# Differential heads: the last keys of a tile by two F32R products of stacked parts, and the norm's squares added by halves

## The chip, the cores and the metric

The kernel runs on one core of one Trainium2 chip. Its engines are named as in the profile: PE is TensorE (the matrix products; PEld is its weight load), DVE is VectorE, ACT is ScalarE, POOL is GpSimd, and SP issues most of the transfers. The metric is the device time of one execution in microseconds (us), as the median of several runs.

## The reference

One block of a streaming encoder, in float32, on 512 tokens of 1024 channels with 16 meta tokens ahead of them (528 positions). The part that matters here is the second branch, differential attention with 8 heads of value width 128:

```
s = einsum('bhcqd,bhckd->bhcqk', q, k) * 64 ** -0.5      # two maps c per head
p = softmax(where(mask, s + bias, -inf))
w = p[:, :, 0] - lam * p[:, :, 1]
o = einsum('bhqk,bhkd->bhqd', w, v)
o = rmsnorm(o, subln_g) * (1 - lam_init)                 # per head and token, over the 128 channels
```

The mask is causal by chunks of 64 tokens. A tile of 128 query tokens therefore sees all positions up to its own end. Since the 16 meta tokens shift the positions, the last 16 keys of a tile lie in the next block of 128 positions, and only the upper 64 query rows of the tile see them. Before this branch comes stick-breaking attention (also 8 heads), and after both a gated merge, an output projection, a SwiGLU and a last norm.

## The kernel before

**Precision.** A product with FP32 operands and one with F32R operands (float32 rounded to a shorter form) are different instructions for TensorE. Nearly all products of the kernel are therefore made in F32R by thirds (`mm3`, L293): each operand is cut into a high part (a copy that rounds, on ACT) and a low part (operand minus high part, on DVE or POOL), and high x high, high x low and low x high are added in PSUM. `split` (L77) makes such a pair: the cast goes to ACT (L78), the subtraction to the engine named (L81). A few small products are left in FP32.

**Order of the work.** Per branch, the heads run in a loop (L1001). A head is a generator (`df_head`, L685) that yields between its steps; at each yield, units of the next head's projections, of finished output projections (`y_units`, L770) and the turning of the next head's values (`turn`, L530) are put in. So PE has other products while the softmax of the head runs on ACT and DVE. Weights come in chunks by SP, are split by ACT and DVE two chunks ahead in this branch (`weights`, L284), and wait in a few buffers. Partial sums of the output projection leave by transfers that POOL issues (L787, L789); POOL also issues the transfers that add weight blocks in the background (L151), one at a time, each behind the last cast made so far. Within these bounds a scheduler orders the instructions of each engine by priority, which follows the program, and by readiness.

**One differential head.** `scores` (L702) and `scores3` (L711) make the logits per query tile, `maps` (L718) the two softmax maps and their difference, in `prs[t]`, queries on partitions. `attn_out` (L550) then has two steps. `turned` transposes the weights' blocks on PE (L563, L564), so that keys lie on partitions; three blocks are cut into high and low parts (L568, L569), the fourth stays FP32 (`a_f`, L570). The last 16 keys of each tile are handled apart: DVE transposes blocks of 32 x 32 (L574), whose last 16 columns are those keys, into `a_s`, which has 32 partitions and 64 columns for each tile. `weighted` adds up the output in one PSUM bank: nine F32R products (L582), one FP32 product of 128 columns with `a_f` (L583), and one FP32 product of 256 columns with `a_s` (L584), which writes the upper 64 columns of each of the four tiles. Its values come from `turn`: `v_s` holds the last 16 positions of each tile in the last 16 of 32 columns, and is transposed on PE (L544) and copied out (L545). The stick-breaking heads use the same functions with 32 query rows instead of 64 (`lo_rows` 96 instead of 64).

**The head's norm.** The output, 128 channels on partitions and 512 tokens in columns, is copied out of PSUM (L751). Its squares are made by POOL (L753), in the last head by DVE, and split into `sqh` (ACT) and `sql` (POOL or DVE) at L754. `norm` (L756) runs inside the next head, after that head's first two score tiles and one unit: two products with a matrix of 1/128 (`ones_r`) add the squares over the partitions (L758, L759), and ACT and DVE make the inverse root and scale the output (L760 to L765). The last head's norm runs after the loop (L1040).

Of the kernel before, what the change touches and what calls it, by code (L numbers as in the profile page):

```python
# [9 lines left out]
F32 = mybir.dt.float32  # L10
F32R = mybir.dt.float32r
BF16 = mybir.dt.bfloat16
AF = mybir.ActivationFunctionType
ALU = mybir.AluOpType
AX = mybir.AxisListType

P = 128
D = 1024
SEQ = 512
NM = 16  # L20
L = NM + SEQ
# [3 lines left out]
NH = 8  # L25
# [16 lines left out]
def block_kernel(ctx: ExitStack, tc: tile.TileContext, x, meta, norm_mix_g, w_in, w_gate, b_gate,  # L42
# [484 lines left out]
    def v_units(key, d):  # L527
        vT = d["vT"] = ap_.tile([P, L], F32, tag="vT", bufs=1, name="vT")

        def turn():  # L530

            vf = ap_.tile([P, 2, P], F32, tag="vf", bufs=2, name="vf")
            vh = ap_.tile([P, 3, P], F32R, tag="vh", bufs=2, name="vh")
            vl = ap_.tile([P, 3, P], F32R, tag="vl", bufs=2, name="vl")
            pt, p5 = tr_tile(), tr_tile()
            for j in range(4):
                nc.tensor.transpose(pt[:, j * P:(j + 1) * P], vT[:, j * P:(j + 1) * P], ident)  # L537
            pv = pt.rearrange("p (j c) -> p j c", c=P)
            nc.scalar.copy(vh, pv[:, 0:3])
            nc.vector.tensor_tensor(vl, pv[:, 0:3], vh.bitcast(F32), op=ALU.subtract)  # L540
            nc.scalar.copy(vf[:, 0], pt[:, 3 * P:4 * P])
            nc.scalar.copy(v_s.rearrange("p (t q) -> p t q", q=32)[:, :, 32 - NM:32],
                           vT[:, NM:L].rearrange("p (t q) -> p t q", q=P)[:, :, P - NM:P])
            nc.tensor.transpose(p5[:, 0:P], v_s, ident)  # L544
            nc.scalar.copy(vf[:, 1], p5[:, 0:P])  # L545
            d["v"] = (vf, vh, vl)

        return kv_units(key, lambda ps, s: nc.scalar.copy(vT[:, s], ps)), turn

    def attn_out(blocks, d, lo_rows):  # L550

        qn = P - lo_rows
        off = (0, 512, 896)
        a_h = ap_.tile([P, 1152], F32R, tag="a_h", name="a_h")
        a_l = ap_.tile([P, 1152], F32R, tag="a_l", name="a_l")
        a_f = ap_.tile([P, P], F32, tag="a_f", name="a_f")

        def turned():
            z0, z1 = z_tile(), z_tile()
            banks = z0[:, 0], z1[:, 0], z0[:, 1]  # L560
            for j, pt in enumerate(banks):
                for t in range(j, NQ):
                    nc.tensor.transpose(pt[:, (t - j) * P:(t - j + 1) * P], blocks(t, j * P, (j + 1) * P), ident)  # L563
            nc.tensor.transpose(z1[:, 1, 0:P], blocks(3, 3 * P, 4 * P), ident)  # L564
            for j, pt in enumerate(banks):
                n = 512 - j * P
                c = slice(off[j], off[j] + n)
                nc.scalar.copy(a_h[:, c], pt[:, 0:n])  # L568
                nc.vector.tensor_tensor(a_l[:, c], pt[:, 0:n], a_h[:, c].bitcast(F32), op=ALU.subtract)  # L569
            nc.scalar.copy(a_f, z1[:, 1, 0:P])  # L570
            for t in range(NQ):
                b = blocks(t, (t + 1) * P - 32 + NM, (t + 1) * P + NM)
                for i in range(qn // 32):
                    nc.vector.transpose(a_s[32 * t:32 * t + 32, t * qn + 32 * i:t * qn + 32 * i + 32],  # L574
                                        b[lo_rows + 32 * i:lo_rows + 32 * i + 32])

        def weighted():
            vf, vh, vl = d["v"]
            ps = z_tile()[:, 0]
            for j in range(3):  # L580
                n = 512 - j * P
                mm3(ps[:, j * P:512], [(vh[:, j], vl[:, j], a_h[:, off[j]:off[j] + n], a_l[:, off[j]:off[j] + n])], j == 0, False)  # L582
            nc.tensor.matmul(ps[:, 3 * P:512], lhsT=vf[:, 0], rhs=a_f, start=False, stop=False)  # L583
            nc.tensor.matmul(ps.rearrange("p (t q) -> p t q", q=P)[:, :, lo_rows:P], lhsT=vf[:, 1],  # L584
                             rhs=a_s[:, 0:4 * qn], start=False, stop=True)
            return ps

        return turned, weighted


# [94 lines left out]
    def df_head(h, d, o_h, o_l):  # L685
        q, k = d["q"], d["k"]
        bias = ap_.tile([P, L], F32, tag="bias", name="bias")
        nc.gpsimd.tensor_scalar(bias, dist, -(2.0 ** -(h + 1)), None, op0=ALU.mult)
        mx = small.tile([P, NQ, 2], F32, tag="mx", name="mx", bufs=2)
        ls = small.tile([P, NQ, 2], F32, tag="ls", name="ls", bufs=2)  # L690
        prs = [ap_.tile([P, 2, 144 + t * P], F32, tag=f"w{t}", name="pr") for t in range(NQ)]

        def score(o, t, c, k0, k1):
            qs = slice(t * P, (t + 1) * P)
            nc.tensor.matmul(o, lhsT=q[c][:, qs], rhs=k[c][:, 0, k0:k1], start=True, stop=False)  # L695
            nc.tensor.matmul(o, lhsT=q[c][:, qs], rhs=k[c][:, 1, k0:k1], start=False, stop=True)  # L696

        def biased(t, c, zz, po, bb):
            nc.vector.tensor_tensor_reduce(po, zz, bb, scale=1.0, scalar=-3.0e38, op0=ALU.add, op1=ALU.max,  # L699
                                           accum_out=mx[:, t, c:c + 1])  # L700

        def scores(t):  # L702
            n = 144 + t * P
            z = z_tile()
            for c in range(2):
                score(z[:, c, 0:max(n, 256)], t, c, 0, max(n, 256))
            for c in range(2):
                biased(t, c, z[:, c, 0:n], prs[t][:, c], bias[:, L - n:L])
            maps(t)

        def scores3(c):  # L711
            two = lambda v: v.rearrange("p (a b) -> p a b", a=2)
            z = z_tile()
            for hf in range(2):
                score(z[:, hf, 0:HL], 3, c, hf * HL, (hf + 1) * HL)
            biased(3, c, z[:, :, 0:HL], two(prs[3][:, c]), two(bias))

        def maps(t):  # L718
            pr = prs[t]
            nm = small.tile([P, 2], F32, tag="nm", name="nm")  # L720
            nc.vector.tensor_scalar(nm, mx[:, t], -1.0, None, op0=ALU.mult)
            for c in range(2):
                nc.scalar.activation(pr[:, c], pr[:, c], AF.Exp, bias=nm[:, c:c + 1], accum_out=ls[:, t, c:c + 1])
            with tc.high_priority(offset=EVAC):
                rc = small.tile([P, 2], F32, tag="rc", name="rc")
                nc.vector.reciprocal(rc, ls[:, t])
                nc.vector.tensor_tensor(rc, rc, cn, op=ALU.mult)
                nc.vector.tensor_scalar(pr[:, 0], pr[:, 0], rc[:, 0:1], None, op0=ALU.mult)
                nc.vector.scalar_tensor_tensor(pr[:, 0], pr[:, 1], rc[:, 1:2], pr[:, 0], op0=ALU.mult, op1=ALU.add)

        scores(0)
        scores(1)
        yield 1
        if late:
            late.pop(0)()
        scores(2)
        yield 1
        scores3(0)
        yield 1
        scores3(1)  # L740
        maps(3)
        turned, av = attn_out(lambda t, k0, k1: prs[t][:, 0, k0:k1], d, 64)
        yield 3 if h < NH - 1 else 2
        turned()
        yield 2
        ps = av()
        of = ap_.tile([P, SEQ], F32, tag="of", name="of")
        sq = ap_.tile([P, SEQ], F32, tag="sq", name="sq")
        sqh = ap_.tile([P, SEQ], F32R, tag="a_h", name="sqh")
        sql = ap_.tile([P, SEQ], F32R, tag="a_l", name="sql")  # L750
        nc.scalar.copy(of, ps)  # L751
        eng = nc.gpsimd if h < NH - 1 else nc.vector
        eng.tensor_tensor(sq, of, of, op=ALU.mult)  # L753
        split(sqh, sql, sq, lo_eng=eng)  # L754

        def norm():  # L756
            pv = tr_tile()
            nc.tensor.matmul(pv, lhsT=ones_r, rhs=sql, start=True, stop=False)  # L758
            nc.tensor.matmul(pv, lhsT=ones_r, rhs=sqh, start=False, stop=True)  # L759
            nc.scalar.activation(sq, pv, AF.Ln, bias=eps_c)  # L760
            cast["norm"] = nc.scalar.activation(sq, sq, AF.Exp, scale=-0.5)
            nc.vector.scalar_tensor_tensor(sq, pv, var_max, sq, op0=ALU.is_le, op1=ALU.mult)
            nc.vector.tensor_tensor(of, of, sq, op=ALU.mult)
            nc.scalar.activation(o_h, of, AF.Copy, scale=g_sub)
            nc.vector.scalar_tensor_tensor(o_l, of, g_sub, o_h.bitcast(F32), op0=ALU.mult, op1=ALU.subtract)  # L765

        late.append(norm)


# [778 lines left out]
```

## Time and profile before

| | us |
|---|---|
| median of 3 runs (lowest to highest) | 931.77 (931.14 to 932.34) |
| the profiled execution | 931.87 |
| its span, first to last instruction | 930.1 |
| DVE busy | 734.3 |
| ACT busy | 586.1 |
| POOL busy | 168.4 |

The profile comes from one execution. Its span leaves out what lies before the first and after the last instruction (1.77 us here). An engine's busy time is the union of its instructions. In a timeline each row is a start, a length, the engine, the source line, what is written and read, and in brackets how long the engine was idle before and what ended that. In the chain of waits, PE's products stand with the time by which the next could follow; in the timeline they stand with their whole length through the array, so that neighbours overlap.

### The profile page before, as it was taken

What the parts mean: (1) busy time and instruction counts of PE and PEld (TensorE: products, weight loads), DVE (VectorE), ACT (ScalarE), POOL (GpSimd) and SP (SyncE); (2) the same over time, 40 slices, a digit from 0 to 9 for tenths busy, and PEclk for the clock granted to TensorE, in tenths of its full rate; (3) what the DMA queues carried; (4) which work ended last, traced back from release to release, by engine and by line L of the source; (5) the groups of instructions that cost most, each with busy time, mean ns of one, the idle gap of its engine ahead of it and who ended that gap; (6) DMA issues with size and microseconds to landing.
All of it is one profiled execution on the core that took longest, in us unless ns stands there. A gap on an engine that the chain in (4) does not pass through costs nothing.

```text
span 930.1 us, 16033 instructions
## 1 busy us (share of the span) xinstructions
PE 918.8 (99%) x6010; PEld 836.9 (90%) x6010; DVE 734.3 (79%) x1413; ACT 586.1 (63%) x1104; POOL 168.4 (18%) x199
## 2 busy tenths in 40 slices
PE   8999999999999999999999999999999999999997
PEld 5999999998999899998988888899999999988886
DVE  7988877776687767976663787899888888799975
ACT  6765676676666666666665555776555555576554
POOL 3000121222333343344512000001100000000013
PEclk9999999999999999999999999999999999999999
DMA  8525598778777878799987774437744343276542
GB/s 253 139 68 168 143 212 201 169 167 250 191 192 177 217 170 182 181 211 186 197 209 181 215 260 159 127 80 183 169 118 131 91 129 98 88 274 193 192 149 91
DMA packets 155823, 158.41 MB, mean 170 GB/s; under 512 B 6465, under 2 KB 117218, under 8 KB 155746
## 3 DMA queue, kind: packets, MB, share of 16 engines
q1 hardware_dynamic: 132690, 101.61, 36.2%
q0 software_dynamic: 22896, 55.72, 29.2%
q8 instruction: 47, 0.77, 0.3%
q14 instruction: 30, 0.25, 0.1%
q10 hardware_dynamic: 160, 0.07, 0.0%
HBM read 133.64 MB, written 50.86 MB: 198 GB/s over the span
## 4 chain that ended last, share of the span: by engine, by line
PE 94%; DVE 3%; ACT 2%; issue 1%; ACTq 0%; DVEq 0%
PE mm L297 22%; PE mm L296 22%; PE mm L298 22%; PE z L297 7%; PE z L296 7%; PE z L298 7%; PE z L563 2%; PE z L696 1%; PE z L695 1%; PE tr L537 1%; DVE wl L81 1%; DVE hres L1205 1%; PE z L584 1%; PE mm L858 0%; ACT wh L78 0%
## 5 line engine op out<-in xcount | busy, mean ns | idle before, releaser
L296 PE MATMUL mm<-xT_h,wh 128*128 128x264 f32 (+2 forms) x656 | 213.6, 326 | 0.5 <-ACT xT_h L901 0.5
L297 PE MATMUL mm<-xT_l,wh 128*128 128x264 f32 (+2 forms) x656 | 213.4, 325 | 0.5
L298 PE MATMUL mm<-xT_h,wl 128*128 128x264 f32 (+2 forms) x656 | 212.5, 324 | 0.0
L78 ACT CAST wh<-wst 128x1024 fp32r<-128x1024 f32 (+1 forms) x147 | 141.5, 967 | 78.8 <-PE mm L297 56.0
L81 DVE TENSOR_TENSOR wl<-wst,wh 128x1024 fp32r<-128x1024 f32 (+1 forms) x147 | 163.1, 1114 | 31.3 <-ACT wh L78 30.9
L297 PEld LDWEIGHTS mm<-xT_l,wh 128*128 128x128 f32 x656 | 123.4, 188 | 10.3 <-DVE xT_l L902 1.3
L298 PEld LDWEIGHTS mm<-xT_h,wl 128*128 128x128 f32 x656 | 123.5, 188 | 10.0
L296 PEld LDWEIGHTS mm<-xT_h,wh 128*128 128x128 f32 x656 | 123.4, 188 | 9.9 <-ACT xT_h L901 0.9
L296 PE MATMUL mm<-hT_h,wh 128*128 128x256 f32 x304 | 84.0, 278 | 0.5 <-ACT hT_h L1162 0.5
L298 PE MATMUL mm<-hT_h,wl 128*128 128x256 f32 x304 | 84.1, 278 | 0.0
L297 PE MATMUL mm<-hT_l,wh 128*128 128x256 f32 x304 | 84.1, 277 | 0.0
L699 DVE CUSTOM_DVE_ANT_0 pr<-z,bias 128x144 f32<-128x144 f32 (+3 forms) x64 | 30.9, 501 | 34.1 <-PE z L696 31.8
L296 PEld LDWEIGHTS mm<-hT_h,wh 128*128 128x128 f32 x304 | 56.9, 188 | 0.8 <-ACT hT_h L1162 0.7
L298 PEld LDWEIGHTS mm<-hT_h,wl 128*128 128x128 f32 x304 | 57.2, 188 | 0.0
L297 PEld LDWEIGHTS mm<-hT_l,wh 128*128 128x128 f32 x304 | 57.0, 188 | 0.0
L296 PE MATMUL mm<-o_h,wh 128*128 128x512 f32 x128 | 52.4, 410 | 0.0
L297 PE MATMUL z<-wl,da 128*128 128x512 f32 (+1 forms) x132 | 50.3, 381 | 0.2 <-DVE wl L81 0.2
L296 PE MATMUL z<-wh,da 128*128 128x512 f32 (+1 forms) x132 | 50.2, 380 | 0.0
L298 PE MATMUL z<-wh,da 128*128 128x512 f32 (+1 forms) x132 | 50.2, 380 | 0.0
L298 PE MATMUL mm<-o_h,wl 128*128 128x512 f32 x128 | 50.1, 391 | 0.0
L297 PE MATMUL mm<-o_l,wh 128*128 128x512 f32 x128 | 49.9, 390 | 0.0
L151 POOL DMA_DIRECT2D ds<-in_w_ffn_down_dram x36 | 30.1, 840 | 92.0 <-ACT wh L78 62.2
(378 smaller groups left out, 2468.0 us busy)
## 6 DMA issues: line engine op xcount, KB each, us to landing
wst<-in_w_in_dram SPq DMA_DIRECT2D x40, 512.0 KB, 5.9
ds<-in_w_ffn_down_dram POOLq DMA_DIRECT2D x30, 512.0 KB, 6.2
wst<-in_w_ffn_gate_dram SPq DMA_DIRECT2D x22, 512.0 KB, 3.9
wsu<-in_w_ffn_up_dram SPq DMA_DIRECT2D x20, 512.0 KB, 3.9
wst<-in_w_gate_dram SPq DMA_DIRECT2D x16, 512.0 KB, 5.5
y_df<-y_out POOLq DMA_DIRECT2D x32, 256.0 KB, 7.2
slots<-ds SPq DMA_DIRECT2D x13, 512.0 KB, 3.2
os<-in_w_out_dram POOLq DMA_DIRECT2D x12, 512.0 KB, 5.0
```

Source lines behind the costliest of these rows:

```text
L78: cast["last"] = (hi_copy or nc.scalar.copy)(hi, src)
L81: cast["lo"] = (lo_eng or nc.vector).tensor_tensor(lo, src, hi.bitcast(F32), op=ALU.subtract)
L151: tc.add_manual_dep(nc.gpsimd.dma_start(dst, src, **kw).ins, cast["last"].ins.name, paced)
L296: nc.tensor.matmul(ps, lhsT=ah, rhs=bh, start=(start and i == 0), stop=False, skip_group_check=skip)
L297: nc.tensor.matmul(ps, lhsT=ah, rhs=bl, start=False, stop=False, skip_group_check=skip)
L298: nc.tensor.matmul(ps, lhsT=al, rhs=bh, start=False, stop=(stop and i == n - 1), skip_group_check=skip)
L537: nc.tensor.transpose(pt[:, j * P:(j + 1) * P], vT[:, j * P:(j + 1) * P], ident)
L563: nc.tensor.transpose(pt[:, (t - j) * P:(t - j + 1) * P], blocks(t, j * P, (j + 1) * P), ident)
L584: nc.tensor.matmul(ps.rearrange("p (t q) -> p t q", q=P)[:, :, lo_rows:P], lhsT=vf[:, 1], rhs=a_s[:, 0:4 * qn], start=False, stop=True)
L695: nc.tensor.matmul(o, lhsT=q[c][:, qs], rhs=k[c][:, 0, k0:k1], start=True, stop=False)
L696: nc.tensor.matmul(o, lhsT=q[c][:, qs], rhs=k[c][:, 1, k0:k1], start=False, stop=True)
L699: nc.vector.tensor_tensor_reduce(po, zz, bb, scale=1.0, scalar=-3.0e38, op0=ALU.add, op1=ALU.max, accum_out=mx[:, t, c:c + 1])
```

## The change

Four things change, all in the differential branch; the stick-breaking heads keep the old form.

- **Values of the last keys.** `v_s` now holds each tile's 16 positions twice, side by side. After the transpose on PE they lie on 32 partitions per tile, and are cut into a high part (ACT) and a low part (DVE), both F32R, in a tile `v_e` that is used by turns by even and odd heads.
- **Weights of the last keys.** For each tile the 16 columns of the last keys are cut into a high (ACT) and a low part (DVE), which are put side by side in `stk`, and this block of 32 columns is transposed by DVE into `a_s`. POOL copies `a_s` into the F32R tile `a_sr`.
- **The product.** The FP32 product of 256 columns becomes two F32R products of 256 columns: high values with the stack, low values with the stack. As each stack holds the high part over the low part, the two add up all four partial products.
- **The norm, heads 0 to 6.** POOL squares channels 64 to 127 into partitions 0 to 63, ACT squares channels 0 to 63, POOL adds the two, ACT casts the sum's high part into partitions 0 to 63 of `sqh` and POOL puts the low part into partitions 64 to 127. One product with `ones_r` then adds all. The last head keeps the old form.

```diff
@@ v_units, turn
+            ends = vT[:, NM:L].rearrange("p (t q) -> p t q", q=P)[:, :, P - NM:P]
+            if key[0] == "df":
+                nc.scalar.copy(v_s.rearrange("p (t a q) -> p t a q", a=2, q=NM),
+                               ends.unsqueeze(2).broadcast_to([P, NQ, 2, NM]))
+            else:
+                nc.scalar.copy(v_s.rearrange("p (t q) -> p t q", q=32)[:, :, 32 - NM:32], ends)
             nc.tensor.transpose(p5[:, 0:P], v_s, ident)
-            nc.scalar.copy(vf[:, 1], p5[:, 0:P])
+            if key[0] == "df":
+                if not ends_of:
+                    ends_of.append(ap_.tile([P, 2, 2, P], F32R, tag="wsu", name="v_e"))
+                vs = [ends_of[0][:, key[1] % 2, i] for i in range(2)]
+                nc.scalar.copy(vs[0], p5[:, 0:P])
+                nc.vector.tensor_tensor(vs[1], p5[:, 0:P], vs[0].bitcast(F32), op=ALU.subtract)
+                d["ends"] = vs
+            else:
+                nc.scalar.copy(vf[:, 1], p5[:, 0:P])
@@ attn_out
+        stacked = lo_rows == 64
+        if stacked:
+            stk = ap_.tile([P, NQ, 2, NM], F32R, tag="lp", name="stk")
+            a_sr = ap_.tile([P, 256], F32R, tag="s21", name="a_sr")
@@ attn_out, turned, after the transposes on PE
+            if stacked:
+                for t in range(NQ):
+                    b = blocks(t, (t + 1) * P, (t + 1) * P + NM)[lo_rows:P]
+                    nc.scalar.copy(stk[lo_rows:P, t, 0], b)
+                    nc.vector.tensor_tensor(stk[lo_rows:P, t, 1], b, stk[lo_rows:P, t, 0].bitcast(F32), op=ALU.subtract)
...
             for t in range(NQ):
-                b = blocks(t, (t + 1) * P - 32 + NM, (t + 1) * P + NM)
+                b = stk[:, t].rearrange("p a q -> p (a q)").bitcast(F32) if stacked else blocks(
+                    t, (t + 1) * P - 32 + NM, (t + 1) * P + NM)
...
+            if stacked:
+                nc.gpsimd.tensor_copy(a_sr, a_s)
@@ attn_out, weighted
-            nc.tensor.matmul(ps.rearrange("p (t q) -> p t q", q=P)[:, :, lo_rows:P], lhsT=vf[:, 1],
-                             rhs=a_s[:, 0:4 * qn], start=False, stop=True)
+            rows = ps.rearrange("p (t q) -> p t q", q=P)[:, :, lo_rows:P]
+            if stacked:
+                hi, lo = d["ends"]
+                nc.tensor.matmul(rows, lhsT=hi, rhs=a_sr, start=False, stop=False)
+                nc.tensor.matmul(rows, lhsT=lo, rhs=a_sr, start=False, stop=True)
+            else:
+                nc.tensor.matmul(rows, lhsT=vf[:, 1], rhs=a_s[:, 0:4 * qn], start=False, stop=True)
@@ df_head, after the copy of the output
-        eng = nc.gpsimd if h < NH - 1 else nc.vector
-        eng.tensor_tensor(sq, of, of, op=ALU.mult)
-        split(sqh, sql, sq, lo_eng=eng)
+        halved = h < NH - 1
+        if halved:
+            A, B = slice(0, 64), slice(64, P)
+            sq2 = ap_.tile([P, SEQ], F32, tag="a_l", name="sq2")
+            nc.gpsimd.tensor_tensor(sq[A], of[B], of[B], op=ALU.mult)
+            nc.scalar.activation(sq2[A], of[A], AF.Square)
+            nc.gpsimd.tensor_tensor(sq[A], sq[A], sq2[A], op=ALU.add)
+            cast["last"] = nc.scalar.copy(sqh[A], sq[A])
+            cast["lo"] = nc.gpsimd.tensor_tensor(sqh[B], sq[A], sqh[A].bitcast(F32), op=ALU.subtract)
+        else:
+            sql = ap_.tile([P, SEQ], F32R, tag="a_l", name="sql")
+            nc.vector.tensor_tensor(sq, of, of, op=ALU.mult)
+            split(sqh, sql, sq)
@@ norm
-            nc.tensor.matmul(pv, lhsT=ones_r, rhs=sql, start=True, stop=False)
-            nc.tensor.matmul(pv, lhsT=ones_r, rhs=sqh, start=False, stop=True)
+            if not halved:
+                nc.tensor.matmul(pv, lhsT=ones_r, rhs=sql, start=True, stop=False)
+            nc.tensor.matmul(pv, lhsT=ones_r, rhs=sqh, start=halved, stop=True)
```

More of the change, by code (lines that the diff above doesn't have):

```diff
@@ L541, in turn @@
             nc.scalar.copy(vf[:, 0], pt[:, 3 * P:4 * P])
-            nc.scalar.copy(v_s.rearrange("p (t q) -> p t q", q=32)[:, :, 32 - NM:32],
-                           vT[:, NM:L].rearrange("p (t q) -> p t q", q=P)[:, :, P - NM:P])
-            nc.tensor.transpose(p5[:, 0:P], v_s, ident)
-            nc.scalar.copy(vf[:, 1], p5[:, 0:P])
+            ends = vT[:, NM:L].rearrange("p (t q) -> p t q", q=P)[:, :, P - NM:P]
[4 more added lines that the diff above has]
+                nc.scalar.copy(v_s.rearrange("p (t q) -> p t q", q=32)[:, :, 32 - NM:32], ends)
+            nc.tensor.transpose(p5[:, 0:P], v_s, ident)
+            if key[0] == "df":
[7 more added lines that the diff above has]
+                nc.scalar.copy(vf[:, 1], p5[:, 0:P])
             d["v"] = (vf, vh, vl)
         return kv_units(key, lambda ps, s: nc.scalar.copy(vT[:, s], ps)), turn
+    ends_of = []
     def attn_out(blocks, d, lo_rows):
@@ L749, in df_head @@
         sqh = ap_.tile([P, SEQ], F32R, tag="a_h", name="sqh")
-        sql = ap_.tile([P, SEQ], F32R, tag="a_l", name="sql")
         nc.scalar.copy(of, ps)
-        eng = nc.gpsimd if h < NH - 1 else nc.vector
-        eng.tensor_tensor(sq, of, of, op=ALU.mult)
-        split(sqh, sql, sq, lo_eng=eng)
+        halved = h < NH - 1
[11 more added lines that the diff above has]
+            split(sqh, sql, sq)
         def norm():
             pv = tr_tile()
-            nc.tensor.matmul(pv, lhsT=ones_r, rhs=sql, start=True, stop=False)
-            nc.tensor.matmul(pv, lhsT=ones_r, rhs=sqh, start=False, stop=True)
+            if not halved:
+                nc.tensor.matmul(pv, lhsT=ones_r, rhs=sql, start=True, stop=False)
+            nc.tensor.matmul(pv, lhsT=ones_r, rhs=sqh, start=halved, stop=True)
             nc.scalar.activation(sq, pv, AF.Ln, bias=eps_c)
```

## The prediction

> **What bounds the kernel now.** I read the page first, then the busy time by stage, then the list of TensorE's waits, then the chain around the two edited products, and last the timelines of the engines that get new work.
>
> ```profile
> span 930.1 us, 16033 instructions
> PE 918.8 (99%) x6010; PEld 836.9 (90%) x6010; DVE 734.3 (79%) x1413; ACT 586.1 (63%) x1104; POOL 168.4 (18%) x199
> ...
> PE   8999999999999999999999999999999999999997
> PEclk9999999999999999999999999999999999999999
> ```
>
> TensorE (PE) is busy in 99% of the span, with the granted clock in the top tenth in every slice. A busy PE only proves something if it is busy with back-to-back work, so the next two views ask whether anything makes it wait. First the stages (columns: window, its length, then busy time and count of PE, PEld, DVE, ACT, POOL, then clock, DMA share and rate):
>
> ```profile
> 260.00:490.00 230.00, 229.90 (x1471) 209.93 (x1470) 169.20 (x457) 152.29 (x342) 87.14 (x95) 1.00 0.85 190
> 490.00:600.00 110.00, 110.00 (x492) 91.04 (x491) 74.57 (x122) 60.39 (x103) 9.10 (x12) 1.00 0.64 189
> 600.00:820.00 220.00, 219.25 (x1903) 218.06 (x1902) 194.65 (x311) 134.94 (x224) 5.78 (x7) 1.00 0.46 122
> ```
>
> The first window is the differential stage, where all edits lie: PE is busy 229.90 of 230.00 us. The two stages after it are as full, so time saved in the first is not handed back by a late transfer that the trace shows. Then all of PE's waits in the whole run:
>
> ```profile
> PE mm L858 <- DVE warm_w L851: 1.2, 1, 1.2
> PE z L896 <- DVE xs L891: 1.2, 2, 0.7
> PE mm L296 <- ACT hT_h L1162: 0.5, 1, 0.5
> PE mm L296 <- ACT xT_h L901: 0.5, 2, 0.2
> PE z L297 <- DVE wl L81: 0.2, 1, 0.2
> ```
>
> None of them names an instruction of the heads 0 to 6 (L858, L896 and L901 are the start, L1162 is after the attention). So in this stage the end is set by the number of columns that PE streams, and each column taken away is taken off the end, as long as what feeds PE stays early.
>
> **What the change removes from PE.** The chain, in order of time (start, length, what), once at the last-keys product of a head and once at the norm of that head:
>
> ```profile
> 397.77 0.12 PE z L298
> 397.88 0.22 PE z L583 x2
> 398.11 0.43 PE z L584 x2
> 398.54 0.23 PE mm L296
> ```
>
> ```profile
> 405.00 0.23 PE tr L758
> 405.23 0.23 PE tr L759
> ```
>
> How often each stands in the run (instruction, count, shortest/middle/longest ns, first and last start, shapes):
>
> ```profile
> L584 PE MATMUL z<-a_s,vf x32: 275/327/382, 58.1 to 483.0; 128*128 128x128 f32 x16, 128*128 128x256 f32 x16
> ```
>
> ```profile
> L758 PE MATMUL tr<-sql,ones_r x8: 390/390/497, 286.5 to 486.2; 128*128 128x512 f32 x8
> ```
>
> Each group here is the work of several heads. In the first row the 16 records of 256 columns are the eight differential heads, two each (the FP32 product runs as a pair, 0.43 us together in the chain). The change puts two F32R products of the same 256 columns in its place; nearest is the F32R product of 256 columns three places before it (L298, 0.12 us). So 8 x (0.43 - 2 x 0.12) = 8 x 0.19 = 1.52 us. The ends: if the strided 4 x 64 output or the following switch cost as much as the old product, the gain is 0; if both products hid wholly, 8 x 0.43 = 3.44 us. I take 1.52, since both stream the shape that was priced at 0.12. The norm loses one of two products of 512 columns in heads 0 to 6 (the eighth keeps both): 7 x 0.23 = 1.61 us, with no other value near. Sum: 1.52 + 1.61 = 3.13 us less on PE, 0.42 a head.
>
> [...]
>
> **The new work and what covers it: the norm.** The sum of squares must be ready when PE reaches the norm. POOL, ACT and PE around one head (start, length, engine, what; in brackets the idle time before):
>
> ```profile
> 399.25 1.04 POOL L753 TENSOR_TENSOR sq<-of 128x512 f32<-128x512 f32 x1 [1.70 <-ACT of L751]
> 401.02 1.30 POOL L81 TENSOR_TENSOR sql<-sq,sqh 128x512 fp32r<-128x512 f32 x1 [0.73 <-ACT sqh L78]
> 402.26 0.86 POOL L789 DMA_DIRECT2D y_df<-y_out  x1
> 402.86 1.35 POOL L151 DMA_DIRECT2D ds<-in_w_ffn_down_dram  x1
> 403.43 1.70 POOL L789 DMA_DIRECT2D y_df<-y_out  x1
> ```
>
> ```profile
> 398.58 0.59 ACT L751 COPY of<-z 128x512 f32<-128x512 f32 x1 [0.92 <-PE z L584]
> 400.32 0.62 ACT L78 CAST sqh<-sq 128x512 fp32r<-128x512 f32 x1 [1.16 <-POOL sq L753]
> 400.85 0.58 ACT L785 COPY y_out<-mm 128x512 f32<-128x512 f32 x1
> 401.32 1.05 ACT L78 CAST wh<-wst 128x1024 fp32r<-128x1024 f32 x1
> 402.28 0.58 ACT L785 COPY y_out<-mm 128x512 f32<-128x512 f32 x1
> ```
>
> ```profile
> 404.84 0.39 PE L758 MATMUL tr<-sql,ones_r 128*128 128x512 f32 x1
> ```
>
> ```profile
> L1441 ACT ACTIVATE sq<-hres x9: 416/626/633, 847.0 to 923.7; 128x512 f32<-128x512 f32 x7, 128x256 f32<-128x256 f32 x2
> ```
>
> Now the low part is done at 401.02 + 1.30 = 402.32, and PE wants it at 404.84: 2.52 us early. The change puts an addition between the square and the cast. It has two different operands and 512 elements, as the subtraction has: 1.30 us, and 0.08 to start (from 399.17, the end of the copy, to 399.25). ACT's square of the other half takes about 0.63 (L1441) and runs beside POOL's 1.04. POOL's square goes to half the partitions: between 0.52, if half the rows cost half, and 2.22 (the dearest such row, quoted below); I take 1.04, the row of the same operation. So: square to 400.29, addition 400.37 to 401.67, cast 401.70 to 402.32, subtraction 402.40 to 403.70. Everything after the last-keys product moves earlier by the same amount, so 404.84 - 403.70 = 1.14 us are left, and the edit costs nothing. Should that cover go, each microsecond beyond it costs 7 us.
>
> The waits that come with it: the addition waits for ACT's square, and behind it on POOL stand the issues of L789 and L151, which write partial sums and weight sums that are read in later stages. The cast waits 1.38 us longer; behind it on ACT stand the two y_out copies, which free PSUM banks, and the wh cast for a later weight chunk. Those chunks are made two ahead in this stage, and the wait list has none for them in a differential head, so a delay of 1.4 us stays inside the lead.
>
> **The new work: the last keys.** One head, and the nearest prices:
>
> ```profile
> 391.59 0.42 DVE L574 STREAM_TRANSPOSE a_s<-pr 32x32 f32<-32x32 f32 x2
> ```
>
> ```profile
> 397.94 0.60 PE L584 MATMUL z<-a_s,vf 128*128 128x256 f32 x2
> ```
>
> ```profile
> L542 ACT COPY v_s<-vT 128x64 f32<-128x64 f32 x7 | 1.9, 271 | 0.0
> ```
>
> ```profile
> L727 DVE TENSOR_TENSOR rc<-rc,cn x32: 156/160/163, 256.9 to 475.5; 128x2 f32<-128x2 f32 x32
> ```
>
> ```profile
> L999 POOL MEMSET a_s<- 128x256 f32 x1 | 0.3, 317 | 0.3 <-PE z L584 0.3
> ```
>
> The last query tile's weights are there by 391.59, when its transposes start; the product begins at 397.94. The new chain between them is a small ACT copy (0.27, L542), a small DVE subtraction (0.16, L727), the transposes (0.42) and POOL's cast of 128x256 (0.32 by a fill of that size, at most the 1.30 of a two-operand pass twice as long): 1.17 to 2.15 us in a gap of 6.35. Even behind a wh cast (1.05) and a DMA issue (1.70) it is 1.45 early. The other three tiles come earlier. For the values there is one more DVE subtraction of 128x128 for the next head, a head ahead of its use, which also keeps its PSUM bank until DVE has read it. Per head ACT gets 4 x 0.27 + 0.63 = 1.71 us, DVE 4 x 0.16 and that subtraction (between 0.16 and the 1.22 of a 1024-column split, near the low end), POOL 1.30 and 0.32 to 1.30. Eight heads add at most 14, 15 and 21 us to 152.29, 169.20 and 87.14 busy in 230: none comes near PE.
>
> **Its sum.** The profiled execution took 931.87 us, 1.77 outside its span of 930.1. It would take 931.87 - 3.13 = 928.74. The median of the runs, 931.77, is 0.10 below that execution: 928.64, told as 928.6. About 0.2% (1.86 us) is what a measurement of this kernel can tell from no change, so faster means under 929.9 and slower over 933.6.
>
> **The rivals.** First, **partial cover**. ACT takes the work that is ready at about 401, a y_out copy and the wh cast, before the square's cast. The cast then starts at 402.37 instead of 401.70, or at 402.86 behind the second y_out copy, and the low part is done at 404.37 or 404.86: from 0.47 early to 0.02 late. With one of POOL's issues also ahead of the subtraction, about 0.3 late is likely, 7 x 0.3 = 2.1 us: 930.7. For it: those rows stand exactly in the new gap. Against: the cast comes earlier in the program than they do.
>
> Second, **the other side: POOL and DVE shut each other out**. Late in the run POOL multiplies two tiles while DVE splits weights:
>
> ```profile
> 893.60 2.22 POOL L1450 TENSOR_TENSOR outs<-hres,gF 128x512 f32<-128x512 f32 x1 [0.45 <-DVE hres L1436]
> ```
>
> ```profile
> 893.44 3.46 DVE L81 TENSOR_TENSOR wl<-slots,wh 128x1024 fp32r<-128x1024 f32 x2
> ```
>
> ```profile
> 403.15 1.22 DVE L81 TENSOR_TENSOR wl<-wst,wh 128x1024 fp32r<-128x1024 f32 x1
> ```
>
> A pass that takes 1.30 took 2.22, and two splits of 1.22 took 3.46 instead of 2.44: each waited for the other. A split stands at 403.15 to 404.37 in our head. If the cast slips behind both y_out copies (start 402.86, end 403.48), the subtraction comes to POOL at 403.56, after that split has begun, waits for 404.37 and ends at 405.67: 0.83 late, 7 x 0.83 = 5.81 us, so 928.64 + 5.81 = 934.5. It decides from 1.14 + 3.13 / 7 = 1.59 us of delay, beyond which the kernel is slower than before. For it: POOL reads more in the stage. Against: in the order worked out above the subtraction starts at 402.40, before the split, and then DVE is the one that waits, off the path. [...]
>
> Third, **the products gain nothing**: two F32R products with strided output come out at 0.43 together. Then only the norm's 1.61 remain: 930.2. Against: F32R products in the same accumulation cost 0.12. Fourth, **given back later**: a wait in the later stages takes it up, 931.8. The two full rows above speak against it.
>
> **How the numbers follow.** Forecast 0.73 (928.0 to 929.3). Partial cover 0.11 (929.5 to 932), shut-out 0.07, no gain of the products 0.05, given back 0.04. Faster: the forecast and the mildest partial covers, 0.75. Same: the rest of partial cover, the third and the fourth, 0.18. Slower: 0.07. The range goes from 927.9 (the sum and the runs' own spread of about 0.6) to 930.7, which takes in the middle of partial cover and the third rival; the shut-out, the fourth and half of partial cover stay outside, under 2 in 10.
>
> **What would show it.** Right: the chain gives about 0.24 for the two new products and one 0.23 for the norm; PE's waits name no instruction of the norm; PE's busy time falls by about 3 us and the span with it; POOL's subtraction ends about 1 us before the norm's product. Wrong: an idle time of PE or its weight load at the norm behind POOL, or the last-keys products waiting for POOL's cast; a POOL row of 2 us in a differential head; new waits of PE for wl.

## The result, and the profile after

The changed kernel is slower: 940.68 us (median of 5 runs, 938.87 to 941.76), against 931.14 for the kernel before on the same chip (930.05 to 932.34). The ratio is 1.0091 [1.0075, 1.0107]. The forecast was 928.6, with a range up to 930.7. The profiled execution of the changed kernel took 941.76 us.

The page of the changed kernel, span and busy time:

```profile
span 940.0 us, 16126 instructions
...
PE 920.2 (98%) x6002; PEld 836.8 (89%) x6003; DVE 748.3 (80%) x1453; ACT 598.6 (64%) x1143; POOL 179.6 (19%) x214
```

PE's busy time did not fall (920.2 against 918.8), and the span grew by 9.9 us. The differential stage, as the busy time in the window shown of before:

```profile
260.00:490.00 230.00, 221.93 (x1436) 202.36 (x1435) 180.26 (x493) 160.47 (x374) 98.42 (x110) 1.00 0.84 188
```

PE was busy 229.90 of 230 us here before, now 221.93: it stands still for 8.1 us, at the same clock. The list of PE's waits (total, times, longest) has one new entry at its head:

```profile
PE z L581 <- DVE pr L760: 8.1, 7, 1.4
```

L581 (L563 before) is the first step of `attn_out`: PE transposes the blocks of the softmax weights. L760 (L729 before) is the last DVE instruction of `maps`, which writes the weights of a query tile. So seven times PE waits for the weights, at a place that no step of the prediction looked at. The norm and the last keys, where it did look, are in order. The chain of waits at the last keys (start, length, what):

```profile
401.57 0.22 PE z L609 x2
401.79 0.12 PE z L613
401.91 0.12 PE z L614
```

L613 and L614 are the two new products, 0.12 us each, as priced. And the norm's chain in the same head, first ACT and POOL, then the one product left on PE, from the timelines:

```profile
402.07 0.59 ACT L781 COPY of<-z 128x512 f32<-128x512 f32 x1 [0.61 <-PE z L614]
...
403.46 0.59 ACT L826 COPY y_out<-mm 128x512 f32<-128x512 f32 x1
405.24 0.62 ACT L789 CAST sqh<-sq 64x512 fp32r<-64x512 f32 x1 [1.19 <-POOL sq L788]
```

```profile
402.80 1.04 POOL L786 TENSOR_TENSOR sq<-of 64x512 f32<-64x512 f32 x1 [1.47 <-ACT of L781]
403.93 1.28 POOL L788 TENSOR_TENSOR sq<-sq,sq 64x512 f32<-64x512 f32 x1
405.16 0.85 POOL L830 DMA_DIRECT2D y_df<-y_out  x1
406.08 1.29 POOL L790 TENSOR_TENSOR sqh<-sq,sqh 64x512 fp32r<-64x512 f32 x1
```

```profile
408.35 0.40 PE L800 MATMUL tr<-sqh,ones_r 128*128 128x512 f32 x1
```

The low part is done at 407.37 and used at 408.35: 0.98 us early, where the prediction had 1.14. The order is the predicted one, but for one issue (L830), which lets the subtraction start 0.2 us after the end of the cast (405.86).

### Why PE waits for the weights

First the kernel before, around one pair of transposes: the last weights of a head on DVE, then PE.

```profile
390.25 0.49 DVE L728 TENSOR_SCALAR pr<-pr,rc 128x528 f32<-128x528 f32 x1
390.78 0.77 DVE L729 SCALAR_TENSOR_TENSOR pr<-pr,rc 128x528 f32<-128x528 f32 x1
```

```profile
391.75 1.15 PE L563 MATMUL z<-ident,pr 128*128 128x128 f32 x9
```

The last weights end at 391.55 and the transposes start at 391.75. The fourth of them, 0.32 us after the first, is the first to read the last query tile, so DVE has about half a microsecond in hand. It has no more because DVE has almost no idle time ahead of that point. The busy time of the kernel before, from the first maxima of a head (401.90) to its last weights (421.20), and from there to the next head:

```profile
401.90:421.20 19.30, 19.30 (x137) 18.25 (x136) 18.39 (x54) 12.60 (x30) 8.09 (x9) 1.00 0.99 198
421.20:431.40 10.20, 10.20 (x62) 8.98 (x61) 3.78 (x8) 6.98 (x16) 4.56 (x5) 1.00 1.06 237
```

DVE (the third figure) is busy 18.39 of 19.30 us in the first stretch and 3.78 of 10.20 in the second. The prediction used the mean over the stage, 169.20 of 230, and that mean hides a stretch that is 95% full and ends just before PE needs its result.

The same place after the change, another head:

```profile
423.82 0.17 DVE L587 TENSOR_TENSOR stk<-pr,stk 64x16 fp32r<-64x16 f32 x1
424.02 0.16 DVE L758 TENSOR_TENSOR rc<-rc,cn 128x2 f32<-128x2 f32 x1
424.21 0.20 DVE L598 STREAM_TRANSPOSE a_s<-stk 32x32 f32<-32x32 f32 x1
424.45 0.49 DVE L759 TENSOR_SCALAR pr<-pr,rc 128x528 f32<-128x528 f32 x1
424.98 0.44 DVE L706 SCALAR_TENSOR_TENSOR dk<-mm,dk 64x264 fp32r<-64x264 f32 x1
425.44 0.77 DVE L760 SCALAR_TENSOR_TENSOR pr<-pr,rc 128x528 f32<-128x528 f32 x1
```

```profile
424.60 0.49 PE L581 MATMUL z<-ident,pr 128*128 128x128 f32 x3
426.27 0.87 PE L581 MATMUL z<-ident,pr 128*128 128x128 f32 x6 [1.18 <-DVE pr L760]
```

Three transposes run, and the fourth waits 1.18 us for the weights that end at 426.21. Counted from the first score product of the head, the last weights come 1.4 to 1.5 us later than before (+21.45 to +21.61, against +20.06 to +20.08 in heads 1 to 5), and PE arrives 0.22 to 0.23 us earlier, since the head has one norm product less.

Part of the delay can be read in one row. The sign change of the maxima (`nm`, 128 x 2 elements), before and after (with the maximum that follows it), at the same point of a head:

```profile
402.72 0.17 DVE L721 TENSOR_SCALAR nm<-mx 128x2 f32<-128x2 f32 x1
```

```profile
406.23 1.17 DVE L752 TENSOR_SCALAR nm<-mx 128x2 f32<-128x2 f32 x1
407.31 0.43 DVE L730 CUSTOM_DVE_ANT_0 pr<-z,bias 128x272 f32<-128x272 f32 x1
```

Its row is a microsecond longer, and it ends (407.40) within 0.03 us of POOL's subtraction L790 (406.08 to 407.37, above), which began first. Before, that subtraction was over at 402.32 and `nm` started at 402.72; the longer chain of the norm has moved it onto `nm`. Over the stage, of the 32 instructions with `nm` (shortest/middle/longest ns):

```profile
L752 DVE TENSOR_SCALAR nm<-mx x32: 141/163/1203, 255.2 to 480.0; 128x2 f32<-128x2 f32 x32
```

### The profile page after: what moved, and what is told of

Same layout as the page of the kernel before. It is cut to its first block, busy times and chain, and to the rows that moved or that the text cites. A ratio compares the mean times of both kernels' runs of the same rounds, so it can differ in the third digit from the quotient of the medians.

```text
span 940.0 us, 16126 instructions
## 1 busy us (share of the span) xinstructions
PE 920.2 (98%) x6002; PEld 836.8 (89%) x6003; DVE 748.3 (80%) x1453; ACT 598.6 (64%) x1143; POOL 179.6 (19%) x214
## 4 chain that ended last, share of the span: by engine, by line
PE 75%; DVE 16%; ACT 5%; issue 2%; DMA 1%; DVEq 0%; ACTq 0%
PE mm L296 17%; PE mm L297 17%; PE mm L298 17%; PE z L296 6%; PE z L297 6%; PE z L298 6%; DVE wl L81 3%; ACT pr L754 2%; DVE pr L730 2%; PE z L581 2%; ACT wh L78 1%; DMA wsu<-in_w_ffn_up_dram 1%; DVE nm L752 1%; DVE pr L760 1%; DVE a_s L598 1%
## 5 line engine op out<-in xcount | busy, mean ns | idle before, releaser
L1491 POOL TENSOR_TENSOR outs<-hres,gF 128x512 f32<-128x512 f32 x4 | 6.2, 1548 | 220.5 <-DVE hres L1477 213.4
```

The source lines that it names most:

```text
L1491: nc.gpsimd.tensor_tensor(outs[t][:, D1], hres[:, t, D1], gF[:, D1], op=ALU.mult)
```

## The experiments

The theory: DVE's stretch up to the last weights has almost no slack, and the change lengthens it at two places, by the norm (`nm` held while POOL subtracts) and by the stack's small subtractions on DVE. The rivals: that the wait belongs to one part alone, or that it comes from the order in which work reaches the engines and not from DVE's time.

This table was worked out from the traces by starts of PE's instructions, in us. "Stage" runs from the first score product of the differential heads to the first product of the merge. "Transposes" is the sum of the distances from each of the 72 transposes (L563 or L581) to the next instruction on PE; its excess over 7.85 is waiting (the list of waits counts PE's idle time alone, and so gives less: 8.1 of 9.60 in the changed kernel). "Last weights" is the end of L729 or L760 for the last query tile, from the head's first score product, heads 1 to 6. "Feed-forward" runs from the first to the last product with the hidden rows `hT`.

| kernel | stage | transposes | last weights | feed-forward |
|---|---|---|---|---|
| before | 306.67 | 7.85 | 20.06 to 20.21 | 217.8 |
| after | 313.31 | 17.45 | 21.45 to 21.61 | 220.9 |
| e1_norm_only | 310.90 | 13.70 | 20.95 to 21.11 | 218.7 |
| e2_keys_only | 306.88 | 9.41 | 20.58 to 20.62 | 216.4 |
| e3_keys_held | 309.19 | 7.86 | 19.59 to 19.66 | 216.9 |
| e4_norm_dve | 305.35 | 8.12 | 20.24 to 20.31 | 219.3 |
| e5_one_held | 305.92 | 8.33 | 20.15 to 20.18 | 217.0 |
| e6_one_held_dve | 305.66 | 8.84 | 20.31 to 20.41 | 217.6 |
| e7_nm_act | 312.39 | 15.12 | 21.3 | 218.5 |
| e8_again (after) | 313.34 | 17.43 | 21.45 to 21.61 | 219.2 |
| e9_stack_pool | 304.05 | 8.22 | 19.98 to 20.08 | 217.6 |

**The norm alone.** The changed kernel without the stacked keys:

```diff
-        stacked = lo_rows == 64
+        stacked = False
...
-            if key[0] == "df":
+            if False:
```

> Norm by halves as in the change, last keys as before. Theory (VectorE supplies the last softmax weights just in time, and two separate things push it back: GpSimd's later subtraction shuts VectorE out for 1.0 us at the small negation nm, and the three small subtractions of the stack cost 0.6 us): nm takes about 1.17 us instead of 0.17 in heads 1 to 7, the last weights of a tile come about 1.0 us later than before, TensorE waits about 1.1 us at the transposes of 7 heads, 7.7 us, less the 1.6 us saved: about 937. Rival (all of the loss comes from the stack of the last keys, nm is only slow because the stack's work is late): no wait, 929.5.

Measured: 936.35 us, ratio 1.0057 [1.0038, 1.0077]. The list of PE's waits, and POOL and DVE in one head:

```profile
PE z L581 <- DVE pr L760: 4.3, 7, 0.7
```

```profile
404.14 1.29 POOL L790 TENSOR_TENSOR sqh<-sq,sqh 64x512 fp32r<-64x512 f32 x1
404.28 1.17 DVE L752 TENSOR_SCALAR nm<-mx 128x2 f32<-128x2 f32 x1
```

The same wait is there, and `nm` again ends with the subtraction (405.45 and 405.43). In the table the transposes take 5.85 us more and the stage 4.23, so the norm itself saved 1.62, as forecast (1.61). The time came out as expected (about 937), the wait a little shorter than the 7.7 us that went into it. By itself this part loses.

**The last keys alone.** The changed kernel with the old norm:

```diff
-        halved = h < NH - 1
+        halved = False
...
-            nc.vector.tensor_tensor(sq, of, of, op=ALU.mult)
-            split(sqh, sql, sq)
+            eng = nc.gpsimd if h < NH - 1 else nc.vector
+            eng.tensor_tensor(sq, of, of, op=ALU.mult)
+            split(sqh, sql, sq, lo_eng=eng)
```

> Last keys by two F32R products as in the change, norm as before. Theory: nm at 0.17 us again; three small subtractions of about 0.2 us each ahead of the last weights, less a slack of about 0.1, so a wait of about 0.5 us in 7 heads, 3.5 us, less 1.5 us saved on TensorE: about 933. Rival (the stack is the whole cause): a wait of 1.5 us in each of 7 heads, about 940.

Measured: 932.04 us, ratio 1.0003 [0.9991, 1.0015]: no difference that can be told. No `nm` is held (the longest of the 32 took 0.32 us, as in the kernel before). The last weights come 0.5 us later than before, and the transposes take 1.56 us more. The stage is 0.21 longer, so the products saved 1.35, a little under the 1.52 of the forecast. Both parts delay the last weights on their own (0.9 to 1.0 and 0.5 us), and together by about the sum, 1.4 to 1.5. Of the stack's 0.5 us, DVE's rows account for about 0.3: in heads 1 to 6 three of its four subtractions stand ahead of the last weights (0.52 us together), and five small transposes instead of six (1.01 us against 1.22). The rest comes with the changed order and was not taken apart.

**The stack's high parts held behind the last weights.** The last keys alone, with ACT's four small copies ordered behind the head's last L760, so that nothing of the stack runs in DVE's stretch:

```diff
-                    nc.scalar.copy(stk[lo_rows:P, t, 0], b)
+                    behind(nc.scalar.copy(stk[lo_rows:P, t, 0], b), "maps")
...
-                nc.vector.scalar_tensor_tensor(pr[:, 0], pr[:, 1], rc[:, 1:2], pr[:, 0], op0=ALU.mult, op1=ALU.add)
+                cast["maps"] = nc.vector.scalar_tensor_tensor(pr[:, 0], pr[:, 1], rc[:, 1:2], pr[:, 0], op0=ALU.mult, op1=ALU.add)
```

> As e2_keys_only, but the four casts of the stack wait for the last softmax weights of the head, so that the stack's subtractions and all eight small transposes stand on VectorE behind those weights. Theory: the last weights come about 1 us earlier than in the kernel before (six transposes of 0.2 us leave the stretch), no wait at the transposes of a head, and the 1.5 us saved on TensorE stay: 929.6. Rival (the stack's chain of casts, subtractions, transposes and GpSimd's copy is itself too long for the gap): a wait at the two new products, 931 or more.

Measured: 934.8 us, ratio 1.0032 [1.0021, 1.0044]; the expected gain did not come. The wait at the transposes is gone (7.86), and the weights are 0.4 us earlier than before. But another took its place:

```profile
PE z L296 <- ACT a_f L593: 1.9, 8, 0.3
```

DVE after the last weights of a head, from its timeline:

```profile
392.51 0.26 DVE L587 TENSOR_TENSOR stk<-pr,stk 64x16 fp32r<-64x16 f32 x2
392.80 1.51 DVE L598 STREAM_TRANSPOSE a_s<-stk 32x32 f32<-32x32 f32 x7
394.34 1.23 DVE L81 TENSOR_TENSOR wl<-wst,wh 128x1024 fp32r<-128x1024 f32 x1
395.60 1.56 DVE L592 TENSOR_TENSOR a_l<-z,a_h 128x512 fp32r<-128x512 f32 x3
```

The subtractions and seven of the head's eight small transposes now stand here, ahead of a weight split and of the splits `a_l`; the casts and the copy on ACT that the first weighted product needs come after these. Counted by starts, from the transpose of the next head's values (`v_s`) to that product, this costs 3.3 us over the heads. The stack belongs neither wholly ahead of the last weights nor wholly behind them.

**The norm alone, with its three passes on DVE.** The first experiment with `nc.gpsimd` turned into `nc.vector` at the square, the addition and the subtraction:

```diff
-            nc.gpsimd.tensor_tensor(sq[A], of[B], of[B], op=ALU.mult)
+            nc.vector.tensor_tensor(sq[A], of[B], of[B], op=ALU.mult)
...
-            nc.gpsimd.tensor_tensor(sq[A], sq[A], sq2[A], op=ALU.add)
+            nc.vector.tensor_tensor(sq[A], sq[A], sq2[A], op=ALU.add)
...
-            cast["lo"] = nc.gpsimd.tensor_tensor(sqh[B], sq[A], sqh[A].bitcast(F32), op=ALU.subtract)
+            cast["lo"] = nc.vector.tensor_tensor(sqh[B], sq[A], sqh[A].bitcast(F32), op=ALU.subtract)
```

> As e1_norm_only, but the square, the addition and the low part are made by VectorE, which sits idle for 4 us there, instead of GpSimd. Theory: nm back at 0.17 us, the last weights at most 0.3 us later than before, so between 929.5 (no wait) and 931.5. Rival (the norm costs time because its chain is longer, whatever engine runs it, or because ScalarE's extra square delays the exponentials): still 935 or more.

Measured: 932.0 us, ratio 1.0009 [0.9994, 1.0024], a little above the expected 929.5 to 931.5 and far from the rival's 935. DVE gets two microseconds of work more per head and yet the wait disappears, because that work is done when the head's first maxima start (400.54 and 400.56 in the head shown), and `nm` is no longer held for a microsecond. Its row is 0.40 long here, but the next maximum starts 0.07 us after it; in the changed kernel it starts 1.08 us after (406.23 and 407.31, above). DVE in that head:

```profile
399.85 0.69 DVE L790 TENSOR_TENSOR sqh<-sq,sqh 64x512 fp32r<-64x512 f32 x1 [0.69 <-ACT sqh L789]
400.56 0.31 DVE L730 CUSTOM_DVE_ANT_0 pr<-z,bias 128x144 f32<-128x144 f32 x1
...
401.39 0.40 DVE L752 TENSOR_SCALAR nm<-mx 128x2 f32<-128x2 f32 x1
401.46 0.43 DVE L730 CUSTOM_DVE_ANT_0 pr<-z,bias 128x272 f32<-128x272 f32 x1
```

The stage is 1.32 us shorter than before (1.61 saved, 0.27 lost at the transposes). In its profile the feed-forward stage is 1.5 us longer than that of before and takes this up; more on that below. Against the norm on POOL the stage is 5.55 us shorter, so the cost came with the passes on POOL; that the passes end sooner on DVE is part of the same edit.

**The third tile's stack alone held.** The last keys alone; only the high part of the third tile goes behind the last weights:

```diff
-                    nc.scalar.copy(stk[lo_rows:P, t, 0], b)
+                    hi = nc.scalar.copy(stk[lo_rows:P, t, 0], b)
+                    if t == 2:
+                        behind(hi, "maps")
```

> As e2_keys_only, but only the third tile's cast of the stack waits for the last softmax weights, so that one subtraction of 0.2 us and two transposes of 0.2 us leave VectorE's stretch ahead of those weights. Theory: the last weights come about 0.1 us earlier than in the kernel before, no wait at the transposes of a head and none at the first weighted product, whose low part is late by less than its 1.5 us of room: the 1.5 us saved on TensorE stay, ratio about 0.998. Rival (what e3_keys_held lost comes from holding any of the stack's casts): about 0.4 us of wait in 7 heads, ratio 1.001 or more.

Measured: 930.6 us, ratio 0.9986 [0.9974, 0.9999], a gain just clear of the noise, as expected. The last weights come at about +20.16, 0.1 us later than before where 0.1 earlier was expected, and of the wait one piece is left (0.3 us, in the last head). The third tile's subtraction and transpose are the rows at 423.82 and 424.21 of the changed kernel above: small as they are, they stood in front of the last weights.

**The same, with the norm on DVE.** The changed kernel with the edits of the last two experiments.

> Both parts: the last keys as in e5_one_held, the norm's squares by VectorE as in e4_norm_dve. Theory: the last weights come at most 0.1 us after the time in the kernel before, TensorE wants them 0.23 us earlier and had about 0.4 us of room, so no wait; 3.1 us saved, ratio about 0.9967. Rival (the two parts take the same small room): a wait of 0.1 to 0.3 us in 7 heads, ratio 0.998 to 1.000.

Measured: 931.64 us, ratio 0.9997 [0.9987, 1.0006]; the expected 0.9967 was missed, and what came is the rival's forecast (0.998 to 1.000). The stage is 305.66, 1.0 shorter than before where 3.0 were to be had. The last weights come later than with either part alone (20.31 to 20.41), and the transposes lose 1.0 us. The first weighted product, behind the transpose of `v_s`, loses 0.7, at the same place as in the experiment with all four held; the rest was not traced.

**The sign change on ACT.** The norm alone, on POOL, with `nm` made by ACT:

```diff
-            nc.vector.tensor_scalar(nm, mx[:, t], -1.0, None, op0=ALU.mult)
+            nc.scalar.activation(nm, mx[:, t], AF.Copy, scale=-1.0)
```

> As e1_norm_only, but the negation nm is made by ScalarE. [...] Rival (nm itself was slow for a reason of its own): wl stays at 1.22 us and the last weights come about 1.0 us earlier.

Measured: 937.98 us, ratio 1.0063 [1.0045, 1.0081], no better than the norm alone. The forecast was that the delay passes from `nm` to the next DVE instruction with both operands in SBUF, the split `wl` (from 1.22 to about 1.7 us or more), and that the last weights come 0.3 to 0.6 us earlier than with the norm alone. The first part held, with 1.61 us: in this head the split is the one held up.

```profile
405.68 1.30 POOL L790 TENSOR_TENSOR sqh<-sq,sqh 64x512 fp32r<-64x512 f32 x1
405.98 0.44 DVE L730 CUSTOM_DVE_ANT_0 pr<-z,bias 128x272 f32<-128x272 f32 x1
406.44 1.61 DVE L81 TENSOR_TENSOR wl<-wst,wh 128x1024 fp32r<-128x1024 f32 x1
406.80 0.20 ACT L752 ACTIVATE nm<-mx 128x2 f32<-128x2 f32 x1
```

The split of a weight chunk takes 1.61 us instead of 1.22, while the maximum at 405.98, which reads PSUM and one SBUF tile, keeps its usual 0.44 in the middle of POOL's pass (405.68 to 406.98). But the last weights did not come 0.3 to 0.6 earlier than with the norm alone; they came 0.2 to 0.3 later. `nm` now starts at 406.80, behind a cast and a copy on ACT; how much of the delay this makes was not taken apart. So this run supports that POOL holds DVE, and speaks against `nm` as a special instruction.

**The changed kernel again**, without an edit, for the spread of its stages.

> The changed kernel once more, unedited, for a second profile. Theory: the same wait of about 1.3 us at the transposes of seven heads, to within 0.05 us; the time of the stage with the feed-forward products, 221.1 us in the first profile against 217.9 before, is not made by the change and comes out otherwise. Rival (the change makes that stage longer): 221 again.

Measured: 939.29 us in one execution. The differential stage repeats to 0.03 us, the transposes to 0.02; the feed-forward stage is 1.8 us shorter.

**Both relieved.** The changed kernel with the norm on DVE, as above, and the stack's small subtractions on POOL:

```diff
-                    nc.vector.tensor_tensor(stk[lo_rows:P, t, 1], b, stk[lo_rows:P, t, 0].bitcast(F32), op=ALU.subtract)
+                    nc.gpsimd.tensor_tensor(stk[lo_rows:P, t, 1], b, stk[lo_rows:P, t, 0].bitcast(F32), op=ALU.subtract)
```

> Both savings kept, VectorE relieved at both places: the norm's three passes go from GpSimd to VectorE (nothing of GpSimd's runs beside the maximum's sign change any more), and the four small subtractions of a stack go from VectorE to GpSimd. Theory (VectorE's stretch up to the last weights is what the change lengthens): the last weights come at about +20.25 us after a head's first score product, as with the norm alone on VectorE, so TensorE's waits at the transposes are under 2 us in all instead of 9; the differential stage takes about 304.5 us against 306.7 before (2.7 saved by start-to-start intervals, 0.5 lost), and the time is 0.997 to 0.9995 of before, the upper end if the feed-forward stage again takes about 1.5 us longer than before. Rival (the small subtractions cost through the order of work that they bring, not through their time on VectorE): the last weights stay at +20.6 or later, waits over 3 us, no gain.

Measured: 928.83 us, ratio 0.9977 [0.9964, 0.9991], within the expected 0.997 to 0.9995. It is the fastest version, and faster than both kernels. Its busy time in the stage, its last weights, and its transposes:

```profile
260.00:490.00 230.00, 229.77 (x1474) 209.67 (x1474) 186.10 (x489) 168.11 (x384) 89.59 (x120) 1.00 0.84 191
```

```profile
418.73 0.77 DVE L760 SCALAR_TENSOR_TENSOR pr<-pr,rc 128x528 f32<-128x528 f32 x1
...
419.48 1.15 PE L581 MATMUL z<-ident,pr 128*128 128x128 f32 x9
```

PE is full again (229.77) although DVE is busier than in the slow kernel (186.10 against 180.26). The last weights end at 419.50, the transposes start at 419.48 and run in one piece: the slack that is left is that of the three first transposes. The stage takes 304.05, 2.62 less than before; with the 0.37 lost at the transposes, the two edits save 2.99 us of PE, close to the forecast 3.13. Its rival, that the subtractions cost by the order that they bring, expected the last weights at +20.6 or later, and fell as it was put. But the weights also come 0.25 us earlier than expected (+20.25, as with the norm alone on DVE), and order has a part in that: in heads 1 to 6 only four small transposes stand ahead of them here (0.81 us), against six (1.22) with the norm alone on DVE. So this version shows that relieving the stretch removes the wait, and not how much of it is the subtractions' own time.

**The kernel before, twice more**, without an edit.

> The kernel before once more, for its feed-forward stage. If the spacing of the 256-column products there (113 or 118 ns, for stretches of 10 to 60 us) is a matter of the execution, this profile may show any length between 216.5 and 221 us; if it belongs to the kernel, it shows 217.9 again, within 0.5, as its one profile so far, and stays under the 219.3 to 221.1 of the changed kernel.

> The kernel before a third time, same question: if the feed-forward stage belongs to the kernel, 217.9 within 0.5 once more; if to the execution, 216.5 to 221.

Measured: 932.1 and 933.14 us, one execution each. The differential stage took 306.65 both times, the feed-forward stage 217.9 and 216.3 us, with 217.8 the first time. So that stage changes from one execution to the next, by 1.6 us in this kernel and by 1.8 in the changed one. Whether the changed kernel is slower there on average stays open: its two profiles (219.2 and 220.9) lie above the three of before, and kernels with the new norm lie at 217.6 and above, those with the old one at 217.9 and below. In the first profile of the changed kernel (220.9) the F32R products of 256 columns follow each other every 118 ns in stretches of up to about 60 us, about 110 us in all, and every 113 elsewhere; in the first profile of before (217.8) they do so every 118 for about 45 us in all. The granted clock is shown as 1.00 in both. What causes it was not found.

## Why the prediction was wrong

**The step that failed** stands in two places. "Eight heads add at most 14, 15 and 21 us to 152.29, 169.20 and 87.14 busy in 230: none comes near PE" judged DVE by its mean over the stage. And the second rival was put aside with "the subtraction starts at 402.40, before the split, and then DVE is the one that waits, off the path". DVE is on the path: it finishes the last weights about half a microsecond before PE needs them, the change delays them by 1.4 to 1.5 us, and PE waits 9.60 us in seven heads. The prediction worked out the slack of the norm's product and of the last-keys product, but not that of the step between them which DVE feeds.

The sum, term by term:

- **What PE saves.** Forecast 1.61 for the norm and 1.52 for the products. Measured 1.62 (norm alone) and 1.35 (keys alone), 2.99 together in the fastest version. The terms were right; the products were 0.17 high.
- **The waits.** Forecast 0. Measured 17.45 - 7.85 = 9.60 us at the transposes. 9.60 less 3.0 is 6.6, and the stage grew by 6.64.
- **The rest.** The profiled executions differ by 941.76 - 931.87 = 9.89 us, so 3.2 lie outside the stage, nearly all in the feed-forward stage; in the second profile of the changed kernel the feed-forward stage is 1.4 longer. The medians differ by 9.54 us; if the stage takes 313.3 in every execution, as in both profiles, 2.9 of that lie outside it. This is the open part above.

**The norm's chain** came out as worked out: the subtraction 1.29 long, done 0.98 us early. The first rival (partial cover) did not delay it: ACT did take one y_out copy in the gap (403.46 to 404.05), but then stood idle for 1.19 us until POOL's addition was done, and the wh cast ran behind L789.

**The shut-out rival** had the right engines, and a price for the wrong one. It expected POOL to come second and wait for the weight split; the time it gave, 934.5, was not reached that way. POOL came first, as the main line said, and DVE waited. The subtraction was forecast from 402.40 to 403.70, and the row of `nm` at 402.72 lay in that window; the prediction checked only the split at 403.15 against it. In the changed kernel POOL's subtraction started first (406.08), and `nm` (406.23) took 1.17 us against 0.17. The same stands in all seven heads: each long `nm` (1.03 to 1.20 us) starts 0.14 to 0.29 us after a subtraction L790 and ends 0.03 us after it. What it is in the two engines that holds `nm` was not shown.

**The last keys' chain** was early enough for its own product, as forecast. What was missed is that most of its small instructions (three of four subtractions, five of eight transposes) stand in DVE's queue ahead of the last weights, which come 0.5 us later per head.

**Given back later** was judged by full rows; it may hold in part, and is not settled.

## What to carry to other kernels

For each engine that gets new work, find the next point at which the full engine needs its result, and the busy share of the stretch that ends there; a mean over the stage says nothing about it. When an edit moves a GpSimd pass, look at every VectorE instruction in its new place, the tiny ones too (here `nm`, 128 x 2 elements, went from 0.17 to 1.17 us). And when the saving is a few tenths of a microsecond per head, a part that is moved to an engine with idle time at that point (here, the small subtractions to POOL, the long passes to DVE) decides whether it is kept.

## What was new about the hardware

- A VectorE instruction of 128 x 2 elements took 1.17 us instead of 0.17 while a GpSimd subtraction of 1.29 us ran; seven of 32 took 1.03 to 1.20 us in a run. A maximum that reads PSUM and one SBUF tile was not lengthened by such a pass (0.44 us at 405.98, with the sign change on ACT).
- The reverse, in the experiment with all four copies held: GpSimd's small cast took 1.37 us beside the weight split that began first (394.34 to 395.57), while in the version with the keys alone it took 0.39 (at 394.33, where the split began later, at 394.62).

```profile
394.45 1.37 POOL L601 CAST a_sr<-a_s 128x256 fp32r<-128x256 f32 x1 [3.25 <-DVE a_s L598]
```

- Half the partitions did not make a GpSimd pass cheaper here: the square took 1.04 us on 64 partitions as on 128.
